# A softmax kernel: who issues three early loads, and when the first store may go

## The chip, the cores and the metric

One Trainium2 chip, one core. The time is that of one execution on the device, in microseconds (us). The kernel before takes 160.07 us (median of 3 runs, 160.01 to 160.09).

## What is computed

The input `x` is 16 x 1024 x 512 in float32, 33.55 MB; the output has the same shape. Each row of 512 numbers gets a softmax at temperature 2:

```
x_scaled = x / 2.0
exp_x = exp(x_scaled - max(x_scaled, axis=-1))
out = exp_x / sum(exp_x, axis=-1)
```

The kernel leaves the maximum out in its main path: it takes exp(x/2) and its row sums, and divides. At the end it counts the rows whose sum lies between 1 and 1e30. Only if one doesn't, a second path computes everything again with the maximum. With this input it isn't taken.

## The kernel before

The 16384 rows are spread over 128 partitions, so each partition has 128 rows of 2 KB to work on. They are cut into ten tiles (`TILES`): tile 0 has 3 rows a partition, tile 1 has 5, tiles 2 to 9 have 15 each. A tile's rows lie side by side in memory within a partition, so that a load or a store of a 15-row tile is one piece of 30 KB for each of 128 partitions. All tiles live in one buffer, `arena`, of 98 rows a partition. Tiles 0 to 7 fill it; tiles 8 and 9 take the places of tiles 2 and 3 and can only be loaded when these have been stored (`LATE`).

Each engine has its own list of instructions, written out by hand, and semaphores between them:

- **Loads** (line 125, in `load`). SyncE issues load 0 and ScalarE load 1 in the entry block, ahead of the barrier at which all engines meet at the start (`early`, line 159). ScalarE issues loads 2 to 7 behind that barrier (`loads`, line 163). GpSimd issues loads 8 and 9 (line 184) after the exponentials up to row 83 and when stores 2 and 3 have landed. Tile 1 (`SPREAD`) is loaded in three parts: four rows of all 128 partitions, and the fifth row (the split row) in one transfer for 126 partitions and one for 2.
- **Waits for loads** (line 200). TensorE, which has nothing else to do, waits for each tile's load in order and raises `s_go` for each chunk of the tile.
- **Exponentials** (lines 210 and 278). ScalarE works in chunks of 3, 5 and then always 5 rows. A chunk takes one from `s_go`, runs one `activation` a row with the row's sum beside it, and raises `s_exp` by one. Chunk 8, the first that doesn't belong to tiles 0 to 3, starts at row 38.
- **Division** (lines 172 and 175). VectorE takes up to three chunks at once (a tile of 15 rows): it waits for `s_exp`, takes reciprocals of the sums and multiplies the rows by them, and raises `s_mul`.
- **Stores** (line 143, in `store`). SyncE waits for `s_mul` of a tile and issues its store, in the order 2, 3, 4, 5, 6, 7, 8, 0, 1, 9 (`STORES`). At line 264 it waits for the landing of all.

Of the kernel before, what the change touches and what calls it, by code (L numbers as in the profile page):

```python
# [13 lines left out]
LATE = {8: (2,), 9: (3,)}  # L14
ARENA = 98

FIXED = 8
STORES = (2, 3, 4, 5, 6, 7, 8, 0, 1, 9)

HEAD = [3, 5]  # L20
E = 5

SPREAD = 1
# [8 lines left out]
def kernel(  # L32
# [5 lines left out]
    nc = tc.nc  # L38
# [6 lines left out]
    xf = x.flatten_outer_dims()  # L45
    of = out.flatten_outer_dims()
    N, D = xf.shape
    P = nc.NUM_PARTITIONS
# [17 lines left out]
    tiles, base = [], 0  # L66
# [5 lines left out]
    def dram(ap, t):  # L72
        b, r, _ = tiles[t]
        return ap[b * P : (b + r) * P].rearrange("(p r) d -> p r d", r=r)

    def sb(t):
        _, r, at = tiles[t]
        return arena[:, at : at + r, :]
# [3 lines left out]
    starts = [sum(sizes[:k]) for k in range(len(sizes))]  # L82
# [14 lines left out]
    ld = [nc.alloc_semaphore(f"ld{t}") for t in range(len(tiles))]  # L97
# [3 lines left out]
    s_exp = nc.alloc_semaphore("s_exp")  # L101
# [15 lines left out]
    g_mul = nc.alloc_semaphore("g_mul")  # L117

    def load(eng, t):
        r = tiles[t][1]  # L120
        parts = [(0, P, 0, r)]
        if t == SPREAD:
            parts = [(0, P, 0, r - 1), (0, 126, r - 1, r), (126, P, r - 1, r)]
        for p, q, lo, hi in parts:
            eng.dma_start(  # L125
                out=sb(t)[p:q, lo:hi], in_=dram(xf, t)[p:q, lo:hi]
            ).then_inc(ld[t], 16)

    stored_by = {u: s_home[t] for t, us in LATE.items() for u in us}
    for t, (_, r, at) in enumerate(tiles):  # L130
# [5 lines left out]

    near = STORES[-2]
    sem_of = {**stored_by, near: s_near}
    at_end = landings(t for t in range(len(tiles)) if t not in sem_of)

    def store(eng, t):
        eng.wait_ge(s_mul, upto[t])
        eng.dma_start(out=dram(of, t), in_=sb(t)).then_inc(sem_of.get(t, s_end), 16)

    def take(eng, sem, n):
# [13 lines left out]
    def early():  # L159
        load(nc.sync, 0)  # L160
        load(nc.scalar, 1)

    def loads():
        for t in range(2, min(LATE)):
            load(nc.scalar, t)

    def program():
# [48 lines left out]

        assert sorted(STORES) == list(range(len(tiles)))
        for t in STORES:
            store(nc.sync, t)
# [68 lines left out]
    entry.instructions = []  # L288
    nc.switch_bb("main", None)
    early()  # L290
    first = list(entry.instructions)
    at = next(k for k, i in enumerate(head) if type(i).__name__ == "InstDrain")
    entry.instructions = head[:at] + first + head[at:]
    act = []
    entry.instructions = list(entry.instructions) + [i for i in jumps if i not in act]
    nc.switch_body(here, parent=None, valid_engines=[i.engine for i in jumps])
    loads()
    program()

# [29 lines left out]
```

## Time and profile before

| | |
|---|---|
| median of 3 runs | 160.07 us |
| the profiled execution's own time | 160.08 us |
| its span, from the first to the last instruction | 158.7 us |
| busy: ScalarE, VectorE | 80.4 us, 73.2 us |
| bytes moved by DMA | 67.12 MB, 423 GB/s over the span |
| exponentials, one row: `ACTIVATE` (line 278) | 613 ns, x120 |
| multiplication of a 15-row tile (line 175) | 8.16 us |
| issue of a load by ScalarE (line 125) | 0.24 to 0.67 us, median 0.47 |
| first store issued | 35.17 us |
| last store issued | 133.4 us |

Engines are named as in the profile: DVE is VectorE, ACT ScalarE, POOL GpSimd, SP SyncE, PE TensorE; SPq and ACTq are the instruction queues of SyncE and ScalarE, whose issuing and waiting instructions don't count as busy. Times within the execution are counted from the start of the span. A row for a stretch of time has the stretch, its length, the busy time of PE, PEld, DVE, ACT and POOL with the number of instructions, the granted clock of TensorE, and then the mean busy share of the 16 DMA engines and the GB/s that they moved. Packets are counted where they start, so that a short stretch can show a share over 1. Besides what the page prints, the trace keeps one record for each DMA packet: its queue, start, length and size. A 15-row tile is 128 packets of 30 KB, eight on each of the 16 DMA engines.

### The profile page before, as it was taken

What the parts mean: (1) busy time and instruction counts of PE and PEld (TensorE: products, weight loads), DVE (VectorE), ACT (ScalarE), POOL (GpSimd) and SP (SyncE); (2) the same over time, 40 slices, a digit from 0 to 9 for tenths busy, and PEclk for the clock granted to TensorE, in tenths of its full rate; (3) what the DMA queues carried; (4) which work ended last, traced back from release to release, by engine and by line L of the source; (5) the groups of instructions that cost most, each with busy time, mean ns of one, the idle gap of its engine ahead of it and who ended that gap; (6) DMA issues with size and microseconds to landing.
All of it is one profiled execution on the core that took longest, in us unless ns stands there. A gap on an engine that the chain in (4) does not pass through costs nothing. (4 is left out here: it accounts for less than half of the span.)

```text
span 158.7 us, 671 instructions
## 1 busy us (share of the span) xinstructions
PE 0.2 (0%) x2; PEld 0.1 (0%) x2; DVE 73.2 (46%) x27; ACT 80.4 (51%) x257; POOL 2.2 (1%) x8
## 2 busy tenths in 40 slices
PE   0000000000000000000000000000000000000000
PEld 0000000000000000000000000000000000000000
DVE  0047002989989408920398001990793697000000
ACT  0590699999932991069600598199205980000000
POOL 0000000000000000000200000000000010000000
DMA  7998989899898989898989898989898989898995
GB/s 261 391 488 379 480 387 480 387 464 403 372 495 372 495 372 488 379 488 379 488 379 488 379 488 379 488 379 488 379 488 379 480 387 480 387 480 366 426 490 255
DMA packets 3026, 67.12 MB, mean 423 GB/s; under 512 B 337, under 2 KB 337, under 8 KB 721
## 3 DMA queue, kind: packets, MB, share of 16 engines
q1 hardware_dynamic: 1584, 34.34, 50.5%
q10 hardware_dynamic: 1152, 24.90, 37.1%
q0 software_dynamic: 288, 7.86, 11.5%
q14 instruction: 2, 0.01, 0.0%
HBM read 33.55 MB, written 33.55 MB: 423 GB/s over the span
## 5 line engine op out<-in xcount | busy, mean ns | idle before, releaser
L278 ACT ACTIVATE arena<-arena x120 | 73.5, 613 | 44.2 <-ACTq L146 44.2
L175 DVE TENSOR_TENSOR arena<-arena,recip 128x7680 f32<-128x7680 f32 (+2 forms) x12 | 70.2, 5847 | 0.4
L172 DVE RECIPROCAL recip<-stats 128x15 f32<-128x15 f32 (+2 forms) x12 | 2.7, 224 | 60.1 <-ACT arena L278 50.0
L278 ACT ACTIVATION_READ_ACCUMULATOR arena<-arena x120 | 22.3, 186 | 0.0
L210 ACT ACTIVATE arena<-arena 128x512 f32<-128x512 f32 x8 | 4.9, 616 | 0.0
L206 ACT ACT_TABLE_LOAD x1 | 1.3, 1283 | 5.7 <-issue 5.7
L125 POOL DMA_DIRECT2D arena<-in_x_dram x2 | 1.3, 637 | 75.7 <-ACT arena L278 75.7
L210 ACT ACTIVATION_READ_ACCUMULATOR arena<-arena 128x1 f32 x8 | 1.5, 187 | 0.0
L186 POOL TENSOR_SCALAR inside<-stats 128x128 f32<-128x128 f32 x1 | 0.6, 629 | 50.7 <-ACT arena L278 50.7
L202 PE MATMUL total<-ones,count 128*1 128x1 f32 x2 | 0.2, 164 | 133.6 <-DVE inside L190 133.6
L190 DVE SCALAR_TENSOR_TENSOR inside<-inside,stats 128x128 f32<-128x128 f32 x1 | 0.3, 284 | 0.0
L194 DVE TENSOR_SCALAR flag<-total 1x1 int32<-1x1 f32 x1 | 0.1, 147 | 0.3 <-PE total L202 0.3
L202 PEld LDWEIGHTS total<-ones,count 128*1 128x1 f32 x2 | 0.1, 82 | 133.6 <-DVE inside L190 133.6
L181 POOL MEMSET ones<- 128x1 f32 x1 | 0.1, 98 | 2.2 <-POOLq L40 2.2
L313 POOL MEMSET const-float32-0.0<- 128x1 f32 x1 | 0.1, 104 | 0.2 <-issue 0.2
L313 POOL MEMSET const-bfloat16-1.0<- 128x1 bf16 x1 | 0.1, 107 | 0.0
L313 POOL MEMSET const-uint8-127<- 128x1 uint8 x1 | 0.1, 107 | 0.0
L313 POOL MEMSET const-float32-1.0<- 128x1 f32 x1 | 0.1, 104 | 0.0
L190 DVE DVE_READ_ACCUMULATOR inside<-inside,stats 128x1 f32 x1 | 0.1, 83 | 0.0
## 6 DMA issues: line engine op xcount, KB each, us to landing
out_dram<-arena SPq DMA_DIRECT2D x8, 3840.0 KB, 29.7
arena<-in_x_dram ACTq DMA_DIRECT2D x6, 3840.0 KB, 38.9
arena<-in_x_dram POOLq DMA_DIRECT2D x2, 3840.0 KB, 32.7
out_dram<-arena SPq DMA_DIRECT2D x1, 1280.0 KB, 27.8
arena<-in_x_dram ACTq DMA_DIRECT2D x1, 1024.0 KB
arena<-in_x_dram SPq DMA_DIRECT2D x1, 768.0 KB, 5.6
out_dram<-arena SPq DMA_DIRECT2D x1, 768.0 KB, 25.6
arena<-in_x_dram ACTq DMA_DIRECT2D x1, 252.0 KB
```

What stands on the lines that cost most here:

```text
L125: eng.dma_start(out=sb(t)[p:q, lo:hi], in_=dram(xf, t)[p:q, lo:hi]).then_inc(ld[t], 16)
L172: nc.vector.reciprocal(out=recip[:, b : b + c], in_=stats[:, b : b + c])._wait_ge(s_exp, ks[-1] + 1).then_inc(s_rec, 1)
L175: nc.vector.tensor_mul(out=arena[:, a : a + c], in0=arena[:, a : a + c], in1=recip[:, b : b + c].unsqueeze(2).to_broadcast([P, c, D]),)._w ...
L181: nc.gpsimd.memset(ones[:, :], 1.0).then_inc(s_ones, 1)
L186: nc.gpsimd.tensor_scalar(out=inside[:, :], in0=stats[:, :], scalar1=LO, scalar2=HI, op0=Alu.max, op1=Alu.min,)._wait_ge(s_exp, len(sizes) ...
L190: nc.vector.scalar_tensor_tensor(out=inside[:, :], in0=inside[:, :], scalar=1.0, in1=stats[:, :], op0=Alu.mult, op1=Alu.is_equal, accum_ou ...
L194: nc.vector.tensor_scalar(out=flag[:, :], in0=total[:, :], scalar1=float(N), scalar2=None, op0=Alu.is_ge,)._wait_ge(s_tot, 1).then_inc(s_f ...
L202: nc.tensor.matmul(total[:, :], lhsT=count[:, :], rhs=ones[:, :], start=True, stop=True)._wait_ge(s_cnt, 2).then_inc(s_tot, 1)
L206: nc.scalar.preload_act_table(Exp)
L210: ins = nc.scalar.activation(out=arena[:, b], in_=arena[:, b], func=Exp, scale=0.5, accum_out=stats[:, b : b + 1],)
L278: ins = nc.scalar.activation(out=data, in_=data, func=Exp, scale=0.5, accum_out=stats[:, r : n_rows - E + 1 + r][:, bass.ds(now, 1)],)
L313: nc = _bacc.Bacc("TRN2", target_bir_lowering=False, num_devices=1)
```

## The change

SyncE, and no longer ScalarE, issues the two parts of the split row, right behind load 0. ScalarE issues load 2 behind load 1 in the entry block, ahead of the barrier; loads 3 to 7 remain behind it. Store 2, the first, has a second wait: besides its tile's multiplication it waits until `s_exp` has reached `starts.index(38)`, which is 8, when the exponentials of tile 3 (rows 23 to 37, the fourth tile) are done.

```diff
+HOLD = {2: 38}
...
     def load(eng, t):
-        r = tiles[t][1]
-        parts = [(0, P, 0, r)]
-        if t == SPREAD:
-            parts = [(0, P, 0, r - 1), (0, 126, r - 1, r), (126, P, r - 1, r)]
-        for p, q, lo, hi in parts:
-            eng.dma_start(
-                out=sb(t)[p:q, lo:hi], in_=dram(xf, t)[p:q, lo:hi]
-            ).then_inc(ld[t], 16)
+        r = tiles[t][1] - (t == SPREAD)
+        eng.dma_start(out=sb(t)[:, :r], in_=dram(xf, t)[:, :r]).then_inc(ld[t], 16)
+
+    def spread(eng, t):
+        r = tiles[t][1] - 1
+        for p, q in [(0, 126), (126, P)]:
+            eng.dma_start(out=sb(t)[p:q, r:], in_=dram(xf, t)[p:q, r:]).then_inc(ld[t], 16)
...
     def store(eng, t):
         eng.wait_ge(s_mul, upto[t])
+        if t in HOLD:
+            eng.wait_ge(s_exp, starts.index(HOLD[t]))
         eng.dma_start(out=dram(of, t), in_=sb(t)).then_inc(sem_of.get(t, s_end), 16)
...
     def early():
         load(nc.sync, 0)
         load(nc.scalar, 1)
+        spread(nc.sync, SPREAD)
+        load(nc.scalar, 2)

     def loads():
-        for t in range(2, min(LATE)):
+        for t in range(3, min(LATE)):
             load(nc.scalar, t)
```

## The prediction

> **What bounds the kernel now.** I read the page from the top: the busy shares, the DMA slices, then the queues.
>
> ```profile
> span 158.7 us, 671 instructions
> ...
> PE 0.2 (0%) x2; PEld 0.1 (0%) x2; DVE 73.2 (46%) x27; ACT 80.4 (51%) x257; POOL 2.2 (1%) x8
> ...
> DMA  7998989899898989898989898989898989898995
> ...
> DMA packets 3026, 67.12 MB, mean 423 GB/s; under 512 B 337, under 2 KB 337, under 8 KB 721
> ...
> q1 hardware_dynamic: 1584, 34.34, 50.5%
> q10 hardware_dynamic: 1152, 24.90, 37.1%
> q0 software_dynamic: 288, 7.86, 11.5%
> ```
>
> No compute engine is busy much over half of the span; the DMA engines are, from the first slice to the last (8 and 9 in turn, because packets are counted where they start). The queues' shares add up to 99.1% of 158.73 us, or 157.3 us on each of 16 engines. q1 is SyncE's queue (load 0 and all stores), q10 ScalarE's (loads 1 to 7), q0 GpSimd's (loads 8 and 9). Next, SyncE's own waits:
>
> ```profile
> SPq L143 <- DVE arena L175: 126.7, 8, 32.6
> SPq L264 <- DMA out_dram<-arena: 24.9, 1, 24.9
> ```
>
> The last store is issued at 133.4 and the program then waits 24.9 us for stores alone. The chain of waits therefore stops at the compute that ended at 134; what ends the kernel is the backlog in the DMA queues. Last, the stretches:
>
> ```profile
> 1.00:6.00 5.00, 0.00 (x0) 0.00 (x0) 0.00 (x0) 0.31 (x1) 0.10 (x1) 1.00 0.95 370
> 6.00:8.00 2.00, 0.00 (x0) 0.00 (x0) 0.00 (x0) 1.99 (x4) 0.00 (x0) 1.00 1.11 370
> 8.00:36.00 28.00, 0.00 (x0) 0.00 (x0) 13.46 (x7) 22.61 (x75) 0.00 (x0) 1.00 1.02 439
> 36.00:40.00 4.00, 0.00 (x0) 0.00 (x0) 3.97 (x2) 4.00 (x14) 0.00 (x0) 1.00 0.95 369
> 40.00:62.00 22.00, 0.00 (x0) 0.00 (x0) 14.74 (x5) 14.34 (x48) 0.00 (x0) 1.00 0.99 426
> ```
>
> The last two numbers of a row are the DMA share and GB/s. Reads alone (8 to 36) move 439/1.02 = 430 GB/s per full share; reads and writes mixed (40 to 62) 426/0.99 = 430. So it makes no difference to the rate when stores begin. Two stretches are poor: 6 to 8 gives 370/1.11 = 333, and 36 to 40 gives 369/0.95 = 388. In the packet records the first 30 KB packet of load 2 on each engine takes 1.39 to 1.66 us, and the packet before the first store's 1.30 to 1.66, where all others take 1.14. That is about 0.4 us an engine, twice, and the trace doesn't say why.
>
> The profiled time then is 160.08 = 1.35 outside the span + 1.03 until the first packet + 157.17 of transfers (the last packet ends at 158.20) + 0.53 for its landing and SyncE's last wait. The median of the runs is 160.07, so the profiled run stands for them.
>
> **The change, part by part.** It transfers the same packets: load 1's split row remains 126 and 2 partitions. So only the order of packets, the engine that issues them, and one wait can act.
>
> 1. *Split row on SyncE, load 2 ahead of the barrier on ScalarE.* ScalarE issued load 1 (0.12 to 0.50), the 126-partition part (0.54, 0.67 long), the 2-partition part (1.23, 0.24 long), then drained for the entry barrier at 1.51; load 2 was issued behind the barrier at 2.64, loads 3 to 7 until 5.66, and the table load (1.28) ended at 6.97. Now SyncE issues 0.38 + 0.67 + 0.24 with gaps of 0.04, and drains at about 1.4; ScalarE issues load 1 (0.38) and load 2 (0.36) by 0.9. The barrier's last arrival moves from ScalarE's drain at 1.51 to SyncE's at 1.4, and the work behind it starts 0.1 to 0.2 sooner. Five loads instead of six come then (0.36 to 0.62 each), so the table load ends near 6.3, and tile 0's exponentials, which landed at 5.65, start then and not at 6.98. None of this starts a transfer that the engines lacked: after 2.0 the 1-us stretches show shares of 0.98, 1.01, 1.00 and 0.95, and the records add up to 0.42 of 16 engine-us idle in the microsecond from 4 to 5, which is 0.03 us an engine. The 0.82 between 1 and 2 is load 0's own ramp (engines' first packets start from 1.03 to 1.96) and remains. **Gain: 0 to 0.03; I take 0.03.** If the cover went (load 1 later than 3.1, when load 0's 8 packets of 0.23 are through), each microsecond without packets would cost a microsecond; load 1's first packet comes at 2.51, 0.6 earlier.
>
> 2. *Where the split row now queues.* The records show the queues of an engine alternate packet by packet: from 39.3 one store packet, one load packet, 1.13 apart, and from 2.5 a 6 KB packet of load 0, then an 8 KB one of load 1. In q1 the nine or ten 2 KB packets now follow load 0's eight. When load 0 is through (4.7), four of load 1's packets remain; four small ones pair with these (4 x 0.39, to 6.3), and the other five or six, and up to three semaphore packets, alternate with load 2's (1.14 + 0.08 each): tile 1 lands between 6.3 + 5 x 1.22 + 0.5 = 13 and 6.3 + 9 x 1.16 + 0.5 = 17, not at 8.07. Its exponentials (3.1 us) end at 16 to 20; tile 2's began at 17.38 when its load had landed (16.95). Tiles 2 to 4 are thus between 0.3 us earlier (load 2 lands sooner) and 3.0 later. ScalarE then waits at 45.05 for load 5 anyway, 5.60 us long, which takes up the 3.0. **Cost: 0.** Cover gone, it would be the 3.0.
>
>    [...]
>
> 3. *The hold.* Store 2 waited for tile 2's multiplication (26.99 to 35.15) and was issued at 35.17. Now it also waits for the eighth chunk count of `s_exp`, whose end shows as the start of tile 3's reciprocal at 35.89. Fifteen exponentials (9.2 us) outlast the multiplication beside them (8.16), so the hold binds by 0.7 us in any shift; store 2 goes out at 35.6 to 39.1. Behind it on SyncE's queue is store 3 alone in that time, which is due at 44.36 plus the same shift: not delayed. Waiting for the landing of stores 2 and 3 are GpSimd's loads 8 and 9 (issued at 78.4; store 3 landed at 75.1, and the exponentials of tile 6 ended last). What hides the hold is the load queue: loads 2 to 7 are 23.6 MB, 55 us at 430 GB/s, so without any store the engines would run dry only near 61. The first store's packets now come near 40 to 43. Loads gain in these microseconds what stores lose. At the end store 9 was issued at 133.4 and its packets start near 149, so 15 us of lateness would be hidden there too. **Cost: 0;** without cover, 0.7 to 3.9.
>
> 4. *The two poor stretches.* Load 2's first packets now run among 2 KB ones, and the first store comes later beside other work. No row shows the slow packets in that setting. Bounds: the 0.4 of either goes (-0.4 each), or each of the five or six returns from a 2 KB packet to a 30 KB one costs as much as the one at 6.5 did (+2.0 to +2.5). The nearest rows are the other mixed ones: 6 KB and 8 KB packets in turn cost just their own times (0.23 + 0.31 per pair), and stores 0 and 1 ahead of store 9 show no slow packet at 149. I take 0 and keep both ends.
>
> Sum: 160.08 - 0.03 = **160.05**, no change.
>
> **Rivals.**
> - *Faster: the slow packets at 6.5 go away.* For: they come when 16 engines turn from 2 KB rows to 30 KB rows within 0.6 us, and that common turn is dissolved. Against: the same 0.4 appears at 38 without any 2 KB packet. 160.05 - 0.4 = 159.65.
> - *Slower: the turns between small and large packets cost.* Place: 6 to 17 us, in the alternation of part 2. Price 0.4 a turn, five or six turns: 162.1 to 162.6; if only one more turn costs, 160.5. It decides from the first turn on, since nothing hides DMA time. Against: the mixed rows of part 4. [...]
> - *Slower: the first store's slow packets grow*, because hold and tile 3's multiplication now start together; once more the same 0.4, 160.45.
> - *It doesn't do what it says.* The hold can't fail to bind (part 3); if the split row went ahead of load 1's packets, tile 1 would land as before. Both give 160.05.
>
> **How the numbers follow.** No change 0.68; slow packets gone 0.16; turns cost 0.10; second stretch worse 0.06. Within the first, the engines' last packets end from 157.69 to 158.20: evened out that is worth 0.3, and as much the other way, so 0.02 of it falls beyond 0.2% faster and 0.04 slower. 0.2% (0.32 us) is about what can be told from no change here. Faster 0.18, same 0.62, slower 0.20. The range runs from 159.5 (first rival, with 0.15 from the engines' ends) to 160.7 (one turn, or the second stretch, with 0.2 of the ends); the full price of the turns is left out, with 0.08, and so are tails of the same size.
>
> **What would show it.** Right: tile 1's exponentials starting at 13 to 17; the first store issued 0.4 to 3.9 later than 35.17; a DMA share near 1 from 2 to 157; SyncE's last wait again some 25 us. Wrong: a DMA share clearly below 1 between 2 and 157 (a queue ran dry), 333 GB/s per share in 6 to 8 going to 430 or lasting until 17, or a first packet later than 1.03.

## The result and the profile after

The change makes the kernel a little slower: 160.30 us in the median of 22 runs (160.00 to 160.95), where the kernel before, run beside it, has 160.08 (22 runs, 159.97 to 160.47). The ratio is 1.0016, with a 95% interval from 1.0008 to 1.0023: about 0.26 us lost. That lies within 0.2% and within the range of the prediction, but on the other side of the forecast, which had 0.03 us gained. The fastest runs of both are the same; what the change adds is the upper end. Of its 22 runs 7 are over 160.4, of those of before 2. Of all runs told of here a single one, 164.94 us with 18 added waits, is in a slower state, and it is left out of ratios and counts.

The profiled execution of the changed kernel took 160.57 us, so it is one of the upper ones, 0.49 above that of before. From its page, the span, the DMA slices and the queues:

```profile
span 159.2 us, 672 instructions
...
DMA  7999999999999999989898999999999999999995
...
DMA packets 3025, 67.12 MB, mean 422 GB/s; under 512 B 336, under 2 KB 336, under 8 KB 720
...
q1 hardware_dynamic: 1728, 34.60, 50.9%
q10 hardware_dynamic: 1008, 24.64, 36.4%
q0 software_dynamic: 288, 7.86, 11.5%
```

The split row has gone from q10 to q1 (144 packets: 128 of 2 KB and 16 of 4 bytes), the bytes are the same, and the DMA engines are full from the first slice to the last, as before. Next, what ScalarE and GpSimd waited for, and then SyncE:

```profile
ACT arena L215 <- ACTq L149: 8.8, 1, 8.8
POOL arena L123 <- DMA out_dram<-arena: 5.8, 1, 5.8
```

```profile
SPq L146 <- DVE arena L180: 86.8, 7, 20.1
SPq L145 <- ACT arena L283: 36.3, 1, 36.3
SPq L269 <- DMA out_dram<-arena: 28.5, 1, 28.5
```

ScalarE has a new wait of 8.8 us for tile 1, whose split row lands late. SyncE has a new wait, for the exponentials (line 145 is the hold). At the end SyncE waits 28.5 us for stores and no longer 24.9, since the last store is now issued 3 us earlier, at 130.3, and still nothing ends sooner. The time line has the two dates that moved:

```profile
16.97 0.63 ACT L215 ACTIVATE arena<-arena 128x512 f32<-128x512 f32 x1 [8.85 <-ACTq L149]
```

```profile
38.59 17.95 SPq L146 DMA_DIRECT2D out_dram<-arena  x3
```

Tile 1's exponentials begin at 16.97 (before: 8.84), the first store is issued at 38.59 (before: 35.17). Last, the stretches, with the DMA share and GB/s at the end of each row, of the changed kernel:

```profile
6.00:8.00 2.00, 0.00 (x0) 0.00 (x0) 0.00 (x0) 1.99 (x7) 0.00 (x0) 1.00 1.37 553
8.00:20.00 12.00, 0.00 (x0) 0.00 (x0) 1.93 (x2) 3.15 (x12) 0.00 (x0) 1.00 1.00 414
...
36.00:46.00 10.00, 0.00 (x0) 0.00 (x0) 9.22 (x3) 10.00 (x34) 0.00 (x0) 1.00 1.00 427
```

and the same of the kernel before, as far as the prediction didn't show them:

```profile
8.00:20.00 12.00, 0.00 (x0) 0.00 (x0) 4.95 (x4) 6.61 (x23) 0.00 (x0) 1.00 1.05 451
...
36.00:46.00 10.00, 0.00 (x0) 0.00 (x0) 9.19 (x4) 9.05 (x30) 0.00 (x0) 1.00 0.95 393
```

Per full share, against 430 GB/s: 6 to 8 rises from 333 to 404, 8 to 20 falls from 430 to 414, and 36 to 46 rises from 414 to 427. So one poor stretch is spread over a longer one, and the other all but goes. In sum the mean DMA engine is no later: from the packet records, the last packets of the 16 engines end at 157.85 us in the mean before and at 157.92 after. What differs is how far they lie apart: from 157.69 to 158.21 before, from 157.40 to 158.83 after. Eight engines now end earlier than any did before, and six later than any. (The records don't name an engine; one follows an engine through them by the next packet's start, which is 3 or 4 ns before the last one's end.) The end of the span shows it too, first before, then after:

```profile
157.40:158.70 1.30, 0.00 (x0) 0.00 (x0) 0.00 (x0) 0.00 (x0) 0.00 (x0) 1.00 0.01 0
```

```profile
157.40:158.70 1.30, 0.00 (x0) 0.00 (x0) 0.00 (x0) 0.00 (x0) 0.00 (x0) 1.00 0.12 47
```

Before, no data packet started after 157.4; after, a few engines still started some. **The kernel ends with the slowest of 16 DMA engines, and in the records of both kernels each carries the same share of every 15-row tile (eight packets of 30 KB), so an engine that fell behind was not helped by the others.** In the records the one that ended last at 158.83 took up the first store a packet turn later than most (43.94, against 42.33 to 42.84 for fourteen of them) and lost 0.37 us there, 0.55 at 60 us and 0.49 at 100 us. Two of these three losses no engine of the kernel before has.

So the question for the experiments was which part sets the engines apart, and by what. "Late engines" below are those whose first store packet comes over 0.9 us after the earliest engine's, in the profiled execution.

### The profile page after: what moved, and what is told of

Its sections match the earlier page's. It is cut to its first block, busy times and chain, and to the rows that moved or that the text cites. A ratio compares the mean times of both kernels' runs of the same rounds, so it can differ in the third digit from the quotient of the medians.

```text
span 159.2 us, 672 instructions
## 1 busy us (share of the span) xinstructions
PE 0.2 (0%) x2; PEld 0.1 (0%) x2; DVE 73.2 (46%) x27; ACT 80.3 (50%) x257; POOL 2.2 (1%) x8
## 2 busy tenths in 40 slices
DMA packets 3025, 67.12 MB, mean 422 GB/s; under 512 B 336, under 2 KB 336, under 8 KB 720
```

## The experiments

All were timed in five rounds beside the kernel before. Its own runs in these five batches and beside the change have medians of 160.08 to 160.15, and 25 of 179 are over 160.4.

### The parts one by one

The first four test theory A, that the split row's small packets push the engines out of step, against B, the hold, and C, the early load 2.

The hold alone, on the kernel before (e1):

```diff
     def store(eng, t):
         eng.wait_ge(s_mul, upto[t])
+        if t in HOLD:
+            eng.wait_ge(s_exp, starts.index(HOLD[t]))
```

> The kernel before with the hold alone: all early loads as before, store 2 also waits for tile 3's exponentials. Theory A (the split row's small packets in SyncE's queue alternate with load 2's and push the DMA engines out of step, and the engine that is last sets the end): no loss, 160.1, the sixteen engines' last packets again within 0.5 us of each other, first store issued at 35.9. Theory B (the hold is to blame, since the first store now starts beside other work): the whole loss, about 160.3, last packets up to 1.4 apart.

160.10 us, ratio 1.0006 (0.9994 to 1.0019); 2 of 11 runs over 160.4. First store at 35.95, engines' last packets within 0.53. The hold by itself, at this row, costs nothing that can be told.

The change without the hold (e2):

```diff
-HOLD = {2: 38}
+HOLD = {}
```

> The changed kernel without the hold: split row on SyncE, load 2 ahead of the barrier, store 2 waits for its multiplication alone. Theory A: the whole loss remains, 160.3, last packets of the engines over 1 us apart, tile 1's exponentials at about 17. Theory B: 160.1, last packets within 0.5.

160.16 us, 1.0002 (0.9993 to 1.0011); 0 of 11 over 160.4. The first store went out at 37.77, five engines took it up late, and still the last packets were within 0.69. So the split row's alternation alone is not enough either: the first theory falls as it was put.

The split row alone, with load 2 behind the barrier and no hold (e3, against the change without the hold):

```diff
         spread(nc.sync, SPREAD)
-        load(nc.scalar, 2)
...
-        for t in range(3, min(LATE)):
+        for t in range(2, min(LATE)):
```

> Only the split row moves to SyncE; load 2 stays behind the barrier and there is no hold. Theory A: 160.3 as with the whole change, since load 2's packets start after 6 in any case and meet the small ones there. Theory C (load 2 ahead of the barrier is to blame): 160.1.

160.17 us, 1.0011 (1.0002 to 1.0020); 2 of 11 over 160.4; first store at 36.59, last packets within 0.55. The interval lies just above 1, so this may cost something, though it is less than the whole.

Load 2 alone, ahead of the barrier on ScalarE behind the split row (e4):

```diff
         load(nc.scalar, 1)
+        load(nc.scalar, 2)
...
-        for t in range(2, min(LATE)):
+        for t in range(3, min(LATE)):
```

> Only load 2 moves ahead of the barrier, behind the split row on ScalarE; no hold. Theory A: 160.1, tile 1 lands at about 8 as before, last packets within 0.5 us. Theory C: 160.3.

160.16 us, 1.0004 (0.9995 to 1.0013); 1 of 11 over 160.4. The profiled execution happened to be that one, 160.50, and is of use: fourteen engines took the first store up between 39.15 and 39.82 and lost about 0.45 us each there, two took it up at 41.19 and 41.52 and lost 1.22 and 1.39, and the kernel ended with one of these at 158.78, while the mean engine ended at 157.93. A straggler, an engine that ends well after the rest, is thus not peculiar to the change; by the counts of upper runs it is rarer without it.

### Together, and a longer hold

The change again, unaltered (e5):

> The whole change once more, beside the next three. Alone, none of its parts cost 0.2, so the loss would be theirs together. Theory A2 (the split row's alternation and a later first store together leave some DMA engines a turn behind, and the last engine ends the kernel): again 160.3, single runs up to 160.9, mean end of the engines' last packets near 157.9 as before, the last one 0.8 to 1.5 behind the first. Theory N (the loss was chance): 160.1 and a spread of 0.5.

160.58 us, 1.0021 (1.0010 to 1.0032); 7 of 12 over 160.4. The loss is there again, so it is not chance.

The change with load 2 behind the barrier as in e3, that is, split row and hold (e6):

> The change without its third part: split row on SyncE and hold, but load 2 behind the barrier. Theory A2: 160.3, as the whole change. Theory C2 (it takes load 2 ahead of the barrier too): 160.15. Mean end of the last packets 157.9 by both.

160.30 us, 1.0017 (1.0004 to 1.0030); 5 of 12 over 160.4. Load 2's place doesn't matter; so far, then, split row and hold make the loss together. The mean end was 157.88 in the one profile and 157.86 in the other, the last packets came 1.33 and 1.50 after the first.

A long hold (`HOLD = {2: 68}`), on the kernel before (e7) and on the change (e8):

> The kernel before with a much longer hold: store 2 waits for the exponentials of tile 5 (row 68), near 55, with load 7 the only load still running. Theory D (the DMA engines are kept full whatever is in their queues, so the hold costs nothing until the loads run out near 61): 160.1. Theory B (the hold itself costs, in proportion to its length): well over 160.5.

> The whole change with the hold at row 68. Theory A2 with the mixing of load and store packets as the place where engines fall behind: fewer mixed turns, so 160.1, the last packets within 0.7. Theory B: slower than the change with its own hold, over 160.5.

160.22 us, 1.0004 (0.9991 to 1.0017), and 160.24 us, 1.0002 (0.9992 to 1.0013); 5 and 2 of 12 over 160.4. First stores at 54.23 and 57.00, 19 and 22 us later than before. Neither ratio can be told from 1, so the prediction's cover, the load queue, does what was said of it, and the hold's cost doesn't grow with its length. The 5 of 12 upper runs of the first (the kernel before, run beside it: 6 of 34) leave open whether a first store at 54 is quite free.

### A small shift of the first store

Three versions of the change with 6, 12 and 18 waits on a count already reached, and the kernel before with 12 (e9 to e12):

```diff
-            eng.wait_ge(s_exp, starts.index(HOLD[t]))
+            for _ in range(1 + 6):
+                eng.wait_ge(s_exp, starts.index(HOLD[t]))
```

> The whole change; SyncE passes six more waits that are already met ahead of store 2, so that this store alone goes out some tenths of a microsecond later. Theory P (the loss comes in executions where one or two of the 16 DMA engines take the first store up a packet turn later than the others and are last at the end; which engines do so hangs on when the store comes within a turn of 1.13 us): the number of late engines changes; with 0, or with 5 and more, 160.1; with one or two, 160.4 to 160.8 for the profiled run. Theory H (split row and hold cost 0.3 together, whenever exactly the store comes): 160.3 to 160.5 in the median, as without these waits.

> The same with twelve met waits, about twice the shift, near half a turn. Theory P: late engines 5 or more and 160.1, or 0 and 160.1; Theory H: 160.3 to 160.5.

> The same with eighteen met waits, near a whole turn. Theory P: as the change itself again, one or two late engines and 160.3 to 160.6, if the shift comes to a turn. Theory H: 160.3 to 160.5.

> The kernel before with twelve met waits ahead of store 2, no other change. Theory P: the engines no longer all take the store up in one turn; with one or two late 160.4 and more in single runs, a median of 160.2 to 160.4. Theory H: 160.1, as before.

The shift came to less than was meant: first stores at 38.81, 39.01, 39.09, and 35.45 for the kernel before. The ratios are 1.0012 (0.9999 to 1.0025), 1.0023 (1.0011 to 1.0034), 1.0034 (1.0012 to 1.0055) and 0.9993 (0.9984 to 1.0002); 6 of 12, 6 of 12 and 6 of 11 runs over 160.4, and 0 of 11. Late engines were 5, 10, 14 and 8. So their number follows the shift as the theory had it, and the time does not: with 5 late engines the execution took 160.51, and with 8 of them the kernel before kept its time. The turn in which an engine takes up the first store doesn't decide alone, and this theory falls.

### The pairing of load 8 with store 4

The traces of all kernels with split row and hold at row 38 up to then had something that no other had: between 90 and 112 us 9 to 15 store packets of over 1.20 us, up to 1.40, where 1.14 is the rule. By counting packets: in these kernels load 8 and store 4 run with the same packet number on most engines, and so do load 9 and store 5 after them. If packets of the same number belong to the same partitions, which the records don't show, an engine there writes a partition's new rows and reads its old ones in turn. In the change, every slow packet is on an engine that is paired so, though not every paired engine has them; on engines that are a packet apart there is none. The pairing comes with the wait of GpSimd shown above: load 8 is issued at 74.92, load 9 at 81.45, and not both from 78.39 on as before. First the kernel before, then the change:

```profile
78.39 1.27 POOL L125 DMA_DIRECT2D arena<-in_x_dram  x2 [75.66 <-ACT arena L278]
```

```profile
74.92 0.73 POOL L123 DMA_DIRECT2D arena<-in_x_dram  x1 [72.50 <-ACT arena L283]
81.45 0.53 POOL L123 DMA_DIRECT2D arena<-in_x_dram  x1 [5.81 <-DMA out_dram<-arena]
```

Followed packet by packet, the six engines of the change that end later than any before are of two kinds. Four took the first store up with the rest, then lost 0.5 to 0.7 us each, most of it on paired store packets, and ended from 158.33 to 158.37. The other two took it up a turn late, lost more at 60 and 100 us, and ended at 158.56 and 158.83. By these dates, an estimate: with the pairing alone this execution would have ended some 0.16 later than the one before, and the late engines make the rest of the 0.62. The other profiles of executions over 160.35 show both kinds too. The last engine to end is a late one in e4, e7, e9 and, further on, e16 and e17. In e5 and e6 it is one that was in time, lost 0.3 and 0.5 on paired packets, and lost 0.7 between 153 and 158, where one engine loses 0.44 in the kernel before as well. Being late is not enough: in e8 seven engines were late, and the execution took 159.99.

Four kernels tried the pairing.

Load 8 later in the change (e13, `TURN = 93` in place of 83):

> The whole change, and GpSimd issues load 8 two chunks of exponentials later (row 93, near 81 us and not 74.9). Theory L (store 4 and load 8 running with the same packet number cost the loss): packet numbers differ, no store packet over 1.20 us between 90 and 112, median 160.05 to 160.2, single runs over 160.4 rare. Theory H (split row and hold together, whatever comes later): 160.3 to 160.5 as before.

160.24 us, 1.0021 (1.0006 to 1.0036); 5 of 12 over 160.4. It went further than was meant: loads 8 and 9 were both issued from 90.06 on, and SyncE's last wait for stores fell from 28.5 us to 14.7. The pairing and its slow packets were gone, and the loss in the ratio was not. Since the end of this kernel is arranged anew, its loss need not be the change's.

Load 8 earlier in the kernel before (e14, `TURN = 73`, and e15, `TURN = 78`):

> The kernel before, and load 8 is issued two chunks earlier (row 73, near 72 us and not 78.4); no split row in SyncE's queue and no hold. Theory L: load 8 begins beside store 4's first packets, the same packet numbers, slow store packets between 90 and 112 and a median of 160.25 to 160.5. Theory H: 160.1.

> The kernel before, load 8 one chunk earlier (row 78, near 75 us). Theory L: load 8 begins a packet or two behind store 4, no slow packets, 160.1. Theory H: 160.1. If an early load 8 costs by itself, half of e14's loss.

160.16 us, 0.9997 (0.9988 to 1.0006), and 160.11 us, 0.9993 (0.9983 to 1.0004); none of 11 over 160.4 in either. In the first, load 8 was a packet off store 4 and not level, so that it made no pairing and tells nothing of it.

The change with stores 4 and 5 exchanged (e16, `STORES = (2, 3, 5, 4, 6, 7, 8, 0, 1, 9)`):

> The whole change with stores 4 and 5 in the other order, so that load 8 pairs with store 5 and load 9 with store 4: the same partitions side by side, in DRAM 11.25 and 18.75 MB apart and not 15. If equal partitions in SBUF are the cause: 160.3 to 160.5 and slow packets as before. If the distance in DRAM is: no slow packets and 160.1.

160.29 us, 1.0015 (1.0002 to 1.0028); 4 of 12 over 160.4; 16 slow store packets, up to 1.46. They come with equal packet numbers at other distances in DRAM as well, which speaks against the distance; that it is the partition is not shown. The pairing is real, but since there was a loss without it (the later load 8), it is not shown to be the loss, and hardly is the whole.

### The time of the first store

What the kernels with the loss have in common is then a first store at 38.4 to 39.1 us. The last two have that with one of the two parts each. Split row without hold, and 32 met waits (e17):

```diff
-        eng.wait_ge(s_mul, upto[t])
+        for _ in range(1 + 32 * (t == 2)):
+            eng.wait_ge(s_mul, upto[t])
```

> The changed kernel without the hold; 32 met waits on the multiplication's semaphore bring store 2 from 37.8 to about 38.5 us. Theory T (the first store's time decides, from about 38.4 on): 160.25 to 160.5, 4 or more of some 12 runs over 160.4. Theory I (it takes the hold itself): 160.1 to 160.2, at most 2 runs over 160.4.

160.34 us, 1.0015 (0.9997 to 1.0032); 6 of 12 over 160.4. First store at 38.55. Without these waits it was 0 of 11. But the interval includes 1, and the kernel before had 6 of 20 over 160.4 beside it, so this run alone shows little.

Hold without split row, one chunk later (e18, `HOLD = {2: 43}` on the kernel before):

> The kernel before with a hold one chunk later (row 43), so that store 2 goes out near 39.0 us; the split row stays on ScalarE. Theory T: 160.25 to 160.5, 4 or more of some 12 runs over 160.4. If split row's alternation is needed as well as the late store: 160.1, at most 2 runs over 160.4.

160.79 us, 1.0029 (1.0010 to 1.0047); 5 of 8 over 160.4. Its SyncE waits, and the issue of the first store:

```profile
SPq L146 <- ACT arena L282: 36.3, 1, 36.3
SPq L268 <- DMA out_dram<-arena: 28.1, 1, 28.1
```

```profile
38.99 14.89 SPq L147 DMA_DIRECT2D out_dram<-arena  x3
```

The hold at row 38 on the same kernel (e1), which cost nothing, had its first store 3 us sooner:

```profile
35.95 96.66 SPq L147 DMA_DIRECT2D out_dram<-arena  x10
```

In both, all early loads are as in the kernel before, and the hold alone, one chunk longer, makes the whole loss: the same 36.3 us for the exponentials as in the change, a first store at 38.99, and GpSimd's loads parted as in the change (75.20 and 80.17). The split row is not needed. In these last two kernels the mean engine ended later too, at 158.15 and 158.07. All kernels by the time of the first store:

| first store at | kernels | ratios | runs over 160.4 |
|---|---|---|---|
| 34.9 to 37.8 | a single part, the change without the hold, or the kernel before with 12 waits or an earlier load 8 (7 kernels) | 0.9993 to 1.0011 | 5 of 77 |
| 38.4 to 39.1 | the change twice, and 8 kernels | 1.0012 to 1.0034 | 57 of 125 |
| 54.2, 57.0 | long hold | 1.0004, 1.0002 | 7 of 24 |

The bound of 160.4 was chosen after the first runs were seen; the ratios part the first two rows as well, if barely (1.0011 and 1.0012 at the border). And nine of the ten profiles in the middle row have the pairing of load 8 with store 4 as well, so the table doesn't part the date of the first store from that. The kernel before itself, with its first store at 35.17, has 25 of 179.

## Why the prediction was wrong

**The hold, "Cost: 0", is the step that failed, and with it the sum's single term for what 16 engines transfer.** Held to 38.99, on early loads as before, the first store cost 0.29% (e18); held to 35.95 it cost nothing that can be told (e1). In the change it is the 2.64 us of lateness from part 2, also "Cost: 0", that carry the held store from 35.95 to 38.59. The reason given was that the load queue keeps the engines full until 61. That holds: the shares stay near 1 (1.00 in each of the four stretches of the change from 8 to 90), and a first store at 57 costs nothing clear (ratio 1.0002). But it speaks of the engines together. The sum "1.03 + 157.17 of transfers + 0.53" treated 157.17 as one quantity, though it ends with one engine out of 16, and the mean of their ends (157.85 before, 157.92 after) doesn't tell when the last one ends. The sentence that did carry this, "the engines' last packets end from 157.69 to 158.20: evened out that is worth 0.3, and as much the other way", was given 0.06 in all; the last engine's distance from the mean went from 0.36 to 0.91 us in the profiled executions. With the 0.07 by which the mean moved, the last packet ended 0.62 later; its landing took 0.13 less, and that makes the 0.49 between them. That the median, 160.30, lies within the forecast's range is in the main luck: its upper end was drawn from a slow packet on every engine, which did not come, and only 0.2 of it was for the engines' ends.

Taken by its own steps:

- *Split row and load 2.* Right in what moves: tile 1's exponentials at 16.97 (said: 13 to 17), table load over at 6.2 (6.3), the first 2.33 for work behind the barrier (0.1 to 0.2 sooner than 2.64; it was 0.3). Alone they cost nothing (ratio 1.0002). SyncE's two issues took 0.45 and 0.24, not 0.67 and 0.24.
- *The queue.* The small packets do alternate one by one with load 2's: an engine's records read 2 KB, 30 KB, 2 KB, 30 KB from 6.2 to 13.9, five times. "Cost: 0" for the 3 us by which tiles 2 to 4 are late was wrong only in what came of it, the later first store.
- *The hold's own date.* 35.6 to 39.1 was said, 38.59 measured; it binds, as said, and store 3 behind it went out at 47.01.
- *The poor stretches.* Both rivals came true in part and cancel: load 2's packets among the small ones take 1.16 to 1.25 and not 1.14, some 0.09 more each for five or six turns, and the first of them no longer 1.39 to 1.66. The price of 0.4 a turn was far off (and six such turns would be 2.4, not the 2.5 of the prediction's upper bound). Nothing was gained, as the sum had it.
- *The rival "the first store's slow packets grow"* gave 160.45, near the time of the profiled execution, but not by its mechanism: the mean loss at the first store fell from 0.38 to 0.09 us between these two profiles. It is the uneven part, and the later losses at 60 us and from 92 to 110, that are new.

What is shown: kernels with the first store at 38.4 to 39.1 have the loss, with or without the split row, and those with it at 37.8 or sooner have little or none; the bytes are the same, and in the change the loss is a spread among engines. What is not settled: whether the date itself does it or what comes with it, the pairing above all, and why 38.4 to 39.1 is a bad date, while 37.8 and 57 are not. Nothing was tried between 37.8 and 38.4 nor between 39.1 and 54. The pairing of load 8 with store 4 adds slow packets in nine of the ten profiles with a store at that time (24 and 10 of them in the last two kernels), and the tenth, with the later load 8, has a loss without it; but its profile fell on an execution of 160.21, so what set its engines apart wasn't seen. The records don't name the DMA engine, so it also stays open whether it is always the same one.

## What to carry to other kernels

Where DMA is full from end to end, as here, moving loads and stores about changed no bytes (67.12 MB before and after) and the mean engine's end little (157.77 to 158.15 over these 20 profiles); look then at when each of the 16 engines ends, since the last one set the time (158.83 in the change, against 157.92 in the mean), and at how the median and the upper runs differ, not at the fastest. A wait that is covered on average can still shift one queue against another (the hold at row 43 alone had load 8 issued at 75.20 and load 9 at 80.17, and not both from 78.39 on); judge it by the dates at which queues meet, and try it a chunk earlier and later before ascribing a loss to the part beside it. And one profile of a kernel whose runs lie 0.9 us apart is one draw: parts that looked harmless alone were seen to lose together only by counting runs.

## What was not expected of the hardware

- At the first store after loads alone, each engine of the kernel before lost 0.16 to 0.52 us once (mean 0.38; in the change 0.09), on the load packet just ahead of it; reads and writes in turn then cost nothing (1.14 us a packet). An engine that took the store up late lost up to 1.39 there (load 2 early, 160.50).
- A store and a load that ran with the same packet numbers on one engine came with store packets of over 1.20 us, up to 1.40 in the change and 1.46 with stores 4 and 5 exchanged, in place of 1.14, on some of the engines; on engines a packet apart the change had none.
- From issue to the earliest engine's first packet it took 1.03 us for the first load, and 3.5 to 4.5 us for the first store behind queued loads (35.17 to 39.30 in the kernel before, 38.59 to 42.33 in the change).
- 12 waits already met put off SyncE by about 0.3 us (35.17 to 35.45), 32 by 0.8 (37.77 to 38.55).
